# One layer of a hybrid diffusion backbone: w_out with tokens stationary, x2 and its norm token-major

## The chip, the cores and the metric

The kernel runs on one core of a Trainium2 chip. The metric is the device time of one execution in microseconds. It computes in float32; the matrix products use PE's float32r form with each operand split into a high and a low part, so that one product is three matmuls: high by high, high by low, low by high.

## The reference

One layer, run over 128 context tokens and 256 latent tokens (384 together, D = 2048), which share all weights and differ in their modulation vectors. The mixer (attention, Fourier and gating branches, each behind a sigmoid gate) makes `merged`. What the change touches is the rest:

```
x = x + gt1 * rmsnorm(merged @ w_out, g_post_mix)
h = rmsnorm(x, g_pre_mlp) * (1 + sc2) + sh2
ff = square(relu(h @ w1)) @ w2
x = x + gt2 * rmsnorm(ff, g_post_mlp)
```

`sh1, sc1, gt1, sh2, sc2, gt2` come from silu(c) @ w_ada + b_ada: one row for the context, one for the latents.

## The kernel before

The tokens are three tiles of 128. PE gets all its work from one list, `stream`, of weight pieces of 512 KB or 256 KB: SP's queue loads a piece into one of 4 `raw` buffers, ACT makes the high part `whi` (a CAST) and DVE the low part `wlo` (a subtraction), 4 buffers each; `next_half` hands PE one pair of 512 columns and issues the splits for those ahead. "D" pieces go to a function of their own: those of `w_ada` are multiplied on DVE by silu(c) and summed (`ada_dve`), 96 pieces for gt1, sc2 and sh2, spread over the gates and w_out between places `DL` and `DE` of the main list.

There are two block forms. `blockA` holds the weights stationary and moves the 384 tokens (feature-major result, two tiles of 128 features); `blockB` holds a token tile stationary and moves 512 weight columns (token-major result, three token tiles). After each step `slot` issues at most a few waiting small tasks: `late` (evacuations), `urgent` and `side`.

w_out is eight `blockA` (y0 to y7): ACT squares the result, DVE scales it by `a1` = gt1 * g_post_mix (a value per feature, so per partition) into `ya`, and adds the squares. After the last matmul, column sums and the broadcast of 1/rms go through small PE matmuls (`colsum`, `rstd_bc`, tiles r1c, r1d and r). Then each of 16 feature tiles of x2 = x + ya * r1 is made (`x2_a`), split into high and low parts of A2 * x2 (`x2_b`, `x2_c`), and the first three MLP blocks run beside it, k by k. x comes back from DRAM (`spill`), where it was put feature-major early on.

The second norm is not applied to h2: the MLP's first layer multiplies A2 * x2, with the two shift rows `sh2` as two more moving columns (386), and `ff_evac` multiplies by r2 and adds the shift times w1 as the bias of the Relu. For the end of the kernel x2 is transposed back to token-major, one feature tile at a time, as side tasks of the first MLP blocks (`do_x2`, tile px).

The order on each engine is the order in which the code issues instructions; the Tile framework adds the waits.

Of the kernel before, what the change touches and what calls it, by code (L numbers as in the profile page):

```python
# [22 lines left out]
NT = 3  # L23
# [11 lines left out]
def hybrid_layer_kernel(ctx: ExitStack, tc: tile.TileContext, I: dict, O: dict):  # L35
# [132 lines left out]
    a1 = cst.tile([P, 2, 16], F32, name="a1")  # L168
    st = cst.tile([P, 32], F32, name="st")
    ssq3 = cst.tile([P, NT, 4], F32, name="ssq3")  # L170
# [32 lines left out]
    spill = dram.tile([P, 16, TOK], F32, name="spill")  # L203
# [49 lines left out]
    adr = {}  # L253

    def ada_dve(m, j, kk0, on_done, vec):
        def run(raw):
            if (m, j) not in accs:
                if m in (2, 3, 4):
# [48 lines left out]
    def mod_done(m, j):  # L307
# [12 lines left out]
        def fin():  # L320
            dst = modT[:, m, :, s]
            tt(nc.vector, dst.rearrange("p v (h n) -> p v h n", h=2), last.pop("red")[:, 0:256].rearrange("p (n v h r) -> p v h n r", n=2, v=2, h=2)[:, :, :, :, 0],
               bT[:, m, s].rearrange("p (h n) -> p h n", h=2).unsqueeze(1).to_broadcast([P, 2, 2, 2]), ALU.add)
            if m == 2:
                tt(nc.vector, a1[:, :, s], dst, bc2(g_post_mix[:, s]), ALU.mult)
            if m == 4:
                plus1_times(A2, 4, g_pre_mlp, s)

        return lambda: [red, nop, tr, fin]
# [91 lines left out]
    for p in range(8):  # L421
        main += WA(w_out, KT, 256 * p)
    DL, DE = 62, 196
# [3 lines left out]
    for m in (2, 4, 3):  # L427
        for j in range(4):
            dl += ADA(m, j)
    di = 0  # L430
    for i, e in enumerate(main):
# [4 lines left out]
        while di < want:  # L436
            stream.append(dl[di])
            di += 1
# [156 lines left out]
    def mmA(ps, half, k0, src, first, last_, width=TOK, nk=2):  # L595
# [3 lines left out]
        for kk in range(nk):  # L599
            k = k0 + kk  # L600
            xh = src(0, k)[:, 0:width]
            xl = src(1, k)[:, 0:width]
            s0 = first and kk == 0
            s1 = last_ and kk == nk - 1
            for n in range(len(ps)):
                wh = h3[:, kk, n * P:(n + 1) * P]
                wl = l3[:, kk, n * P:(n + 1) * P]
                mm3(ps[n][:, :width], wh, wl, xh, xl, s0, s1)
# [13 lines left out]
    def blockA(name, src, nkt, evac, k_off=0, width=TOK):  # L622
        ps = [acc_tile(f"{name}_{n}") for n in range(2)]
        for k in range(0, nkt, 2):
            h = next_half()
            mmA(ps, h, k_off + k, src, k == 0, k == nkt - 2, width)
# [77 lines left out]
    def spill_x(k):  # L704
        return lambda: nc.scalar.dma_start(out=spill[:, k:k + 2, :], in_=xT[:, k:k + 2, :])

# [7 lines left out]
    n_spill = KT // 2  # L714
    side.extend(spill_x(2 * i) for i in range(n_spill))
# [389 lines left out]
    yx = area.tile([P, 2, 16, TOK], F32, tag="A", name="yx")  # L1105
    ya = yx[:, 0]
    xr = yx[:, 1]
    for k in range(0, KT, 2):
        side.extend([nop] * 5)
        side.append(lambda k=k: nc.sync.dma_start(out=xr[:, k:k + 2, :], in_=spill[:, k:k + 2, :]))  # L1110
    ysum = {}

    def y_sq(p, ps, n):
        def run():
            k = 2 * p + n
            if k == 0:
                ysum["t"] = tp.tile([P, TOK], F32, tag="ta", name="sqa", bufs=1)
                nc.scalar.activation(out=ysum["t"], in_=ps[n][:, :TOK], func=AF.Square)
            else:
                sq = tp.tile([P, TOK], F32, tag="sq", name=f"ysq{k}")  # L1120
                nc.scalar.activation(out=sq, in_=ps[n][:, :TOK], func=AF.Square)
                if k >= KT - 2:
                    ysum["pair"].append(sq)
                else:
                    tt(nc.vector, ysum["t"], ysum["t"], sq, ALU.add)
        return run

    def y_sc(p, ps, n):
        def run():
            k = 2 * p + n  # L1130
            for v, lo, hi in SEG:
                nc.vector.tensor_scalar(out=ya[:, k, lo:hi], in0=ps[n][:, lo:hi], scalar1=a1[:, v, k:k + 1],
                                        scalar2=None, op0=ALU.mult)
        return run

    def y_evac(p):
        return lambda ps: [f(p, ps, n) for f in (y_sq, y_sc) for n in range(2)]

    for p in range(7):
        blockA(f"y{p}", src_m, KT, y_evac(p))  # L1140
    def colsum(pc, sq, first, last_):
        for t in range(NT):
            nc.tensor.matmul(pc[:, t:t + 1], sq[:, t * P:(t + 1) * P], ones[:, 0:1], start=first, stop=last_)
# [12 lines left out]
    ysum["pair"] = []
    for n in range(2):
        for kk in range(2):
            k = KT - 2 + kk
            mm3(ps7[n][:, :TOK], hi[:, kk, n * P:(n + 1) * P], lo[:, kk, n * P:(n + 1) * P], src_m(0, k), src_m(1, k),  # L1160
                False, kk == 1)
        if n:
            tt(nc.vector, ysum["t"], ysum["t"], ysum["pair"][0], ALU.add)
            colsum(pc1[:, 0:NT], ysum["t"], True, True)
            nc.vector.tensor_scalar(out=st[:, 4:7], in0=pc1[:, 0:NT], scalar1=1.0 / D, scalar2=EPS,
                                    op0=ALU.mult, op1=ALU.add)
        y_sq(7, ps7, n)()
    pc2 = mis_tile("r1d")
    colsum(pc2[:, 0:NT], ysum["pair"][1], True, True)
    rsqrt_add(st[:, 0:3], pc2[:, 0:3], st[:, 4:7], 3, D)  # L1170
    for n in range(2):
        y_sc(7, ps7, n)()
    r1 = mis_tile("r1")
    rstd_bc(r1, st[:, 0:3])
    while urgent or side:
        (urgent or side).popleft()()
    assert not delayed and state["done"] >= mlp_start
    h2t = [area.tile([P, 2, 8, 388], F32R, tag="B1", name="h2a"),
           area.tile([P, 2, 4, 388], F32R, tag="B2a", name="h2b"),
           area.tile([P, 2, 4, 388], F32R, tag="B2b", name="h2c")]  # L1180
# [198 lines left out]
```

## Time and profile before

| | |
|---|---|
| median of three runs | 2188.98 us (2188.03 to 2190.05) |
| profiled execution | 2191.05 us, span 2189.3 us |
| PE busy, granted clock | 99%, 0.996 of full |
| DVE, ACT, POOL busy | 63%, 38%, 2% |
| HBM | 178 GB/s over the span |

A matmul's printed duration runs from its start to its result, and the next one starts before that: the pitch is read from one start to the next. The chain of waits goes back from the last instruction and says which engine held the end at each time.

### The profile page before, as it was taken

What the parts mean: (1) busy time and instruction counts of PE and PEld (TensorE: products, weight loads), DVE (VectorE), ACT (ScalarE), POOL (GpSimd) and SP (SyncE); (2) the same over time, 40 slices, a digit from 0 to 9 for tenths busy, and PEclk for the clock granted to TensorE, in tenths of its full rate; (3) what the DMA queues carried; (4) which work ended last, traced back from release to release, by engine and by line L of the source; (5) the groups of instructions that cost most, each with busy time, mean ns of one, the idle gap of its engine ahead of it and who ended that gap; (6) DMA issues with size and microseconds to landing.
All of it is one profiled execution on the core that took longest, in us unless ns stands there. A gap on an engine that the chain in (4) does not pass through costs nothing.

```text
span 2189.3 us, 30886 instructions
## 1 busy us (share of the span) xinstructions
PE 2160.6 (99%) x11647; PEld 1986.8 (91%) x11647; DVE 1374.3 (63%) x2366; ACT 830.5 (38%) x1620; POOL 52.0 (2%) x78
## 2 busy tenths in 40 slices
PE   7999999999999999999999999999999999999998
PEld 3679989999999999999999988999889998899986
DVE  3546765557888878888695666786334444344454
ACT  3333344533333333333355433444333443344341
POOL 0000211000000000000000000000000000000000
PEclk9999999999999999999999999999999999999999
DMA  8897853336667677677634566665444444444352
GB/s 309 283 313 263 249 163 120 106 116 211 205 215 212 206 221 214 207 219 228 189 99 134 156 204 208 202 199 157 135 125 125 126 125 130 131 125 125 126 173 77
DMA packets 285558, 390.47 MB, mean 178 GB/s; under 512 B 16517, under 2 KB 184689, under 8 KB 285025
## 3 DMA queue, kind: packets, MB, share of 16 engines
q1 hardware_dynamic: 275952, 372.82, 54.3%
q0 software_dynamic: 3264, 8.91, 1.5%
q10 hardware_dynamic: 6192, 6.77, 0.9%
q8 instruction: 91, 1.49, 0.3%
q14 instruction: 59, 0.48, 0.1%
HBM read 381.09 MB, written 8.28 MB: 178 GB/s over the span
## 4 chain that ended last, share of the span: by engine, by line
PE 97%; issue 1%; DMA 1%; DVE 1%; ACT 0%; POOL 0%; DVEq 0%; POOLq 0%; ACTq 0%
PE m L592 8%; PE m L593 8%; PE m L591 8%; PE z L614 7%; PE z L616 7%; PE z L615 7%; PE g L591 6%; PE g L593 6%; PE g L592 6%; PE b L591 2%; PE y L591 2%; PE b L593 2%; PE b L592 2%; PE y L592 2%; PE y L593 2%; PE sc L247 2%
## 5 line engine op out<-in xcount | busy, mean ns | idle before, releaser
L64 DVE TENSOR_TENSOR wlo<-raw,whi 128x512 fp32r<-128x512 f32 x908 | 615.9, 690 | 622.9 <-ACT whi L70 619.2
L70 ACT CAST whi<-raw 128x512 fp32r<-128x512 f32 x908 | 559.0, 621 | 996.8 <-PE z L616 282.6
L614 PE MATMUL z<-whi,ff 128*128 128x512 f32 x720 | 280.4, 389 | 0.0
L616 PE MATMUL z<-whi,ff 128*128 128x512 f32 x720 | 280.1, 389 | 0.0
L615 PE MATMUL z<-wlo,ff 128*128 128x512 f32 x720 | 280.1, 389 | 0.0
L591 PE MATMUL g<-hA,whi 128*128 128x384 f32 x768 | 259.0, 337 | 0.0
L593 PE MATMUL g<-hA,wlo 128*128 128x384 f32 x768 | 256.8, 334 | 0.0
L592 PE MATMUL g<-hA,whi 128*128 128x384 f32 x768 | 256.7, 334 | 0.0
L279 DVE SCALAR_TENSOR_TENSOR adr<-raw,silT,adr 128x512 f32<-128x512 f32 x360 | 246.5, 746 | 0.0
L591 PE MATMUL m<-h2a,whi 128*128 128x386 f32 x512 | 175.6, 343 | 2.1 <-ACT h2a L1198 2.1
L592 PE MATMUL m<-h2a,whi 128*128 128x386 f32 x512 | 174.9, 342 | 0.2 <-DVE h2a L1202 0.2
L593 PE MATMUL m<-h2a,wlo 128*128 128x386 f32 x512 | 174.6, 341 | 0.0
L614 PEld LDWEIGHTS z<-whi,ff 128*128 128x128 f32 x720 | 135.1, 188 | 28.7 <-issue 0.8
L616 PEld LDWEIGHTS z<-whi,ff 128*128 128x128 f32 x720 | 135.1, 188 | 28.1
L615 PEld LDWEIGHTS z<-wlo,ff 128*128 128x128 f32 x720 | 135.1, 188 | 27.9
L591 PEld LDWEIGHTS g<-hA,whi 128*128 128x128 f32 x768 | 144.2, 188 | 2.9 <-issue 2.9
L592 PEld LDWEIGHTS g<-hA,whi 128*128 128x128 f32 x768 | 144.2, 188 | 0.0
L593 PEld LDWEIGHTS g<-hA,wlo 128*128 128x128 f32 x768 | 144.2, 188 | 0.0
L591 PEld LDWEIGHTS m<-h2a,whi 128*128 128x128 f32 x512 | 97.7, 191 | 3.3 <-ACT h2a L1198 2.4
L592 PEld LDWEIGHTS m<-h2a,whi 128*128 128x128 f32 x512 | 97.9, 191 | 0.8 <-DVE h2a L1202 0.6
L593 PEld LDWEIGHTS m<-h2a,wlo 128*128 128x128 f32 x512 | 97.5, 190 | 0.0
L592 PE MATMUL m<-h2c,whi 128*128 128x386 f32 x256 | 87.2, 341 | 0.0
(351 smaller groups left out, 3622.1 us busy)
## 6 DMA issues: line engine op xcount, KB each, us to landing
raw<-in_w_mlp_dram SPq DMA_DIRECT2D x244, 512.0 KB, 3.7
raw<-in_w_in_dram SPq DMA_DIRECT2D x156, 512.0 KB, 3.9
raw<-in_w_ada_dram SPq DMA_DIRECT2D x128, 512.0 KB, 4.6
erb<-in_w_ada_dram SPq DMA_DIRECT2D x37, 512.0 KB, 7.1
raw<-in_w_out_dram SPq DMA_DIRECT2D x32, 512.0 KB, 4.4
era<-in_w_ada_dram SPq DMA_DIRECT2D x27, 512.0 KB, 5.2
era<-in_w_in_dram SPq DMA_DIRECT2D x20, 512.0 KB, 5.7
raw<-in_w_br_a_dram SPq DMA_DIRECT2D x16, 512.0 KB, 3.8
```

Source lines behind the costliest of these rows:

```text
L64: eng.tensor_tensor(out=out, in0=a, in1=b, op=op)
L70: nc.scalar.copy(out=hi, in_=full)
L247: nc.tensor.matmul(ps[g:g + 2, :wd], silT[:, :, k], r, start=k < 4, stop=k >= KT - 4)
L279: nc.vector.scalar_tensor_tensor(out=acc[v], in0=r, scalar=vec[:, v, k:k + 1], in1=acc[v], op0=ALU.mult, op1=ALU.add)
L591: nc.tensor.matmul(out, wh, xh, start=start, stop=False)
L592: nc.tensor.matmul(out, wh, xl, start=False, stop=False)
L593: nc.tensor.matmul(out, wl, xh, start=False, stop=stop)
L614: nc.tensor.matmul(ps[t], xh, hi, start=first, stop=False)
L615: nc.tensor.matmul(ps[t], xh, lo, start=False, stop=False)
L616: nc.tensor.matmul(ps[t], xl, hi, start=False, stop=last_)
```

## The change

- **w_out:** three `blockB` of 512 columns (y0 to y2), a block of 256 columns over all tokens (y3), and the last 256 columns (y4) one token tile at a time. Nine tenths of y4's weights are split ahead into a buffer of their own (`y_entry`). ACT sums the squares with its accumulator, DVE multiplies by a1 as a row.
- **a1:** is now needed along the free dimension. After gt1's pieces of a column block are summed, the block is transposed, written to DRAM and read back broadcast over the partitions (`back1`, `back2`, tile a1b). gt1's pieces now come last of the three, and all 96 end eight places earlier (`DE` 188).
- **x:** is loaded token-major from the inputs; the spill is gone.
- **Norms:** x2 is made token-major (`x2_f`), its squares summed, x2 scaled by 1/rms into h2's place (`hn_f`), transposed on PE (`tr_f`) and given scale and shift from per-partition scalars, then split (`ev_f`). x2 is copied by DMA to its own buffer for the end.
- **MLP:** the first layer reads 384 columns; `ff_evac` is a Relu without bias or factor. The first four weight halves are held and used once per token tile with 128 moving columns (`m0`).

The diff, cut to its core:

```diff
-    for p in range(8):
-        main += WA(w_out, KT, 256 * p)
-    DL, DE = 62, 196
+    for n in range(3):
+        main += WB(w_out, 0, KT, 512 * n)
+    main += WA(w_out, KT, 1536)
+    for i in range(3):
+        main.insert(len(main) - 14 + 4 * i, y_entry(4 * i))
+    main.append(("W", w_out, 12, 4, 1792, 256))
+    DL, DE = 62, 188
...
-    for m in (2, 4, 3):
+    for m in (4, 3, 2):
+        if m == 2:
+            dl += [None] * 5
...
+    def y4_fin(t):
+        sq = tp.tile([P, 512], F32, tag="sq", name=f"ysq{t}")
+        nc.scalar.activation(out=sq[:, 0:256], in_=ps4[t], func=AF.Square, accum_out=ssq1[:, t, 4:5])
+        y_sc(ps4[t], t, c4)()
+        rsqrt_add(st[:, t:t + 1], ssq1[:, t, 4:5], st[:, 3 + t:4 + t], 1, D)
+
+    def x2_f(t):
+        for n in range(4):
+            c = slice(512 * n, 512 * (n + 1))
+            nc.vector.scalar_tensor_tensor(out=ya[:, t, c], in0=ya[:, t, c], scalar=st[:, t:t + 1], in1=xr[:, t, c],
+                                           op0=ALU.mult, op1=ALU.add)
+            nc.scalar.activation(out=xr[:, t, c], in_=ya[:, t, c], func=AF.Square, accum_out=ssq2[:, t, n:n + 1])
+
+    def r2_f(t):
+        nc.vector.tensor_reduce(out=st[:, 6 + t:7 + t], in_=ssq2[:, t, :], axis=AX.X, op=ALU.add)
+        rsqrt_mean(st[:, 9 + t:10 + t], st[:, 6 + t:7 + t], 1, D)
+
+    def hn_f(t):
+        for n in range(4):
+            c = slice(512 * n, 512 * (n + 1))
+            nc.scalar.activation(out=xr[:, t, c], in_=ya[:, t, c], func=AF.Copy, scale=st[:, 9 + t:10 + t])
...
+    y4(0, range(KT), True, True)
     flush()
...
+    y4_fin(0)
+    x2_f(0)
+    y4(1, range(KT), True, True)
+    r2_f(0)
+    hn_f(0)
+    y4_fin(1)
+    x2_f(1)
+    k2 = (12, 13, 14, 15) + tuple(range(12))
+    y4(2, k2[:9], True, False)
+    tr_f(0, 0)
+    y4(2, k2[9:], False, True)
...
+    first = [(0, 0), (0, 1), (0, 2), (2, 0)]
+    while len(halves) < len(first):
+        advance()
+    held = [halves.popleft() for _ in first]
+
+    def m0(t):
+        for (k, p), h in zip(first, held):
+            mmA(ps0[p], h, k, src_h2, k == 0 and t == 0, False, slice(t * P, (t + 1) * P))
+
+    ev_f(0, 0)
+    y4_fin(2)
+    x2_f(2)
+    r2_f(1)
+    hn_f(1)
+    m0(0)
+    tr_f(1, 0)
+    ev_f(1, 0)
+    tr_f(0, 1)
+    r2_f(2)
+    hn_f(2)
+    ev_f(0, 1)
+    m0(1)
+    tr_f(2, 0)
+    ev_f(2, 0)
+    tr_f(1, 1)
+    ev_f(1, 1)
+    m0(2)
+    tr_f(2, 1)
+    ev_f(2, 1)
+    for t in range(NT):
+        nc.gpsimd.dma_start(out=x2[:, t, :], in_=ya[:, t, :])
+    fill = deque((t, g) for g in (2, 3) for t in range(NT))
     for k in range(2, KT, 2):
         for p in range(NJ):
+            if (k, p) in first:
+                continue
+            if fill and hn_t:
+                ev_f(*next(iter(hn_t)))
+            mmA(ps0[p], next_half(), k, src_h2, False, k == KT - 2)
+            if fill:
+                tr_f(*fill.popleft())
...
-                blockA(f"m{qd}{p}", src_h2, KT, ff_evac(p), width=386)
+                blockA(f"m{qd}{p}", src_h2, KT, ff_evac(p))
```

How the order moves, first on PE at the hand-over. The order there before (mH and mL are the parts of `merged`, r1c, r1d and r the small matmuls of the norm, h2a the MLP's input):

```order
L593 MATMUL y_1_10049<-mH,wlo_1_10136 128x384
L1143 MATMUL r1c<-ones,sqa 128x1 x3
L1143 MATMUL r1d<-ones,ysq_10207 128x1 x3
L1147 MATMUL r_10219<-ident,st 128x128 x3
L591 MATMUL m_0_10235<-h2a,whi_0_10165 128x386
```

and now, where y4's third token tile ends:

```order
L656 MATMUL y_2_9968<-wyB2b,mH 128x256
L657 MATMUL y_2_9968<-wyB2b,mH 128x256
L658 MATMUL y_2_9968<-wyB2b,mL 128x256
L633 MATMUL m_0_10168<-h2a,whi_0_9956 128x128
L634 MATMUL m_0_10168<-h2a,whi_0_9956 128x128
L635 MATMUL m_0_10168<-h2a,wlo_0_9957 128x128
L633 MATMUL m_1_10169<-h2a,whi_0_9956 128x128
```

The norm's small matmuls are gone from PE, the first four transposes of h stand earlier, 21 matmuls before y4's end, and the first MLP matmuls have 128 columns.

On ACT in the same place, now (ysq and L1199 are the squares of y and x2, L1208 the copies that scale x2, whi the weight splits, h2a the high part of h2):

```order
L1190 ACTIVATE ysq_10029,ssq_95<-y_0_9966 128x256
L1199 ACTIVATE yx,ssq_96<-yx 128x512 x4
L1208 ACTIVATE yx<-yx,st 128x512 x4
L1190 ACTIVATE ysq_10097,ssq_95<-y_1_9967 128x256
L1199 ACTIVATE yx,ssq_96<-yx 128x512 x4
L70 CAST whi_0_10176<-raw_9908 128x512
L70 CAST whi_0_10182<-raw_9954 128x512
L70 CAST h2a<-hf_10186 128x4x128
L1190 ACTIVATE ysq_10193,ssq_95<-y_2_9968 128x256
```

The first high part of h2 stands behind two token tiles of squares, one of copies and two weight splits.

On DVE, the same stretch from the second token tile on (a1b is the a1 row, hf the scaled and shifted h before its split):

```order
L64 TENSOR_TENSOR yx<-y_1_9967,a1b 128x256
L188 SCALAR_TENSOR_TENSOR st<-ssq_95,st 128x1
L1197 SCALAR_TENSOR_TENSOR yx<-yx,st 128x512 x4
L64 TENSOR_TENSOR wlo_0_10177<-raw_9908,whi_0_10176 128x512
L64 TENSOR_TENSOR wlo_0_10183<-raw_9954,whi_0_10182 128x512
L1229 TENSOR_SCALAR hf_10186<-hn_10137,A_92,modT 128x128 x4
L64 TENSOR_TENSOR h2a<-hf_10186,h2a 128x4x128
```

The first h2 group stands behind the second tile's x2 and two low weight parts.

## Rows read from the trace of the kernel before

**Rows 1.** The page, parts 1 and 4: busy time of the engines; the chain of waits.

```profile
PE 2160.6 (99%) x11647; PEld 1986.8 (91%) x11647; DVE 1374.3 (63%) x2366; ACT 830.5 (38%) x1620; POOL 52.0 (2%) x78
...
PE 97%; issue 1%; DMA 1%; DVE 1%; ACT 0%; POOL 0%; DVEq 0%; POOLq 0%; ACTq 0%
```

**Rows 2.** Timeline of PE in w_out (start us, us, engine, line, operation): 25 matmuls.

```profile
1079.75 0.33 PE L591 MATMUL y<-mH,whi 128*128 128x384 f32 x1
...
1083.91 0.33 PE L591 MATMUL y<-mH,whi 128*128 128x384 f32 x1
```

**Rows 3.** The same in the second MLP layer: 28 matmuls.

```profile
2129.67 0.39 PE L615 MATMUL z<-wlo,ff 128*128 128x512 f32 x1
...
2135.79 0.39 PE L615 MATMUL z<-wlo,ff 128*128 128x512 f32 x1
```

**Rows 4.** The same, last quarter of the first MLP layer: its start, its successor.

```profile
1914.13 0.33 PE L591 MATMUL m<-h2a,whi 128*128 128x386 f32 x1
...
2049.86 0.40 PE L614 MATMUL z<-whi,ff 128*128 128x512 f32 x1
```

**Rows 5.** Timeline of the hand-over from w_out to the MLP.

```profile
1095.17 0.34 PE L593 MATMUL y<-mH,wlo 128*128 128x384 f32 x1
...
1098.40 1.65 PE L1147 MATMUL r<-ident,st 128*128 128x128 f32 x6 [1.19 <-POOL st L187]
...
1102.12 0.69 PE L591 MATMUL m<-h2a,whi 128*128 128x386 f32 x1 [2.07 <-ACT h2a L1198]
...
1157.62 0.34 PE L591 MATMUL m<-h2a,whi 128*128 128x386 f32 x1
```

**Rows 6.** Windows: length, busy PE, PEld, DVE, ACT, POOL, granted clock, DMA share, GB/s.

```profile
1098.00:1099.00 1.00, 0.60 (x3) 0.60 (x4) 0.94 (x6) 0.00 (x0) 0.34 (x1) 0.67 0.00 0
...
1107.00:1108.00 1.00, 1.00 (x5) 1.00 (x5) 1.00 (x4) 0.84 (x3) 0.00 (x0) 0.50 0.73 205
...
1109.00:1110.00 1.00, 1.00 (x7) 1.00 (x6) 1.00 (x3) 0.52 (x2) 0.00 (x0) 1.00 0.31 80
```

**Rows 7.** Loads (ns min/median/max), and pieces of the chain with small matmuls (us).

```profile
L288 PEld LDWEIGHTS sum<-adr,ones x96: 106/108/109, 545.9 to 1065.3; 128*32 128x32 f32 x96
...
L591 PEld LDWEIGHTS y<-mH,whi x256: 186/188/189, 958.9 to 1094.7; 128*128 128x128 f32 x128
...
1152.22 0.56 PE r L1143 x6
...
1155.00 0.67 PE r L1147 x6
...
1159.90 0.33 PE px L1245 x3
...
446.03 0.67 PE pg L994 x6
```

**Rows 8.** Timeline of the last norm of the kernel, a chain of the same kind.

```profile
2159.68 0.60 ACT L1260 ACTIVATE zl<-accn 128x512 f32<-128x512 f32 x1 [4.81 <-DVE accn L64]
...
2160.44 0.16 DVE L186 SCALAR_TENSOR_TENSOR st<-ssq,st 128x1 f32<-128x1 f32 x1
...
2160.75 0.57 POOL L187 TENSOR_TENSOR st<-st,mhalf 128x1 f32<-128x1 f32 x1 [654.38 <-DVE st L186]
...
2161.36 2.08 DVE L1330 SCALAR_TENSOR_TENSOR accn<-accn,st,xT 128x512 f32<-128x512 f32 x3 [0.76 <-POOL st L187]
```

**Rows 9.** Groups by line: busy us, mean ns, idle before and its releaser.

```profile
L64 DVE TENSOR_TENSOR wlo<-raw,whi 128x512 fp32r<-128x512 f32 x908 | 615.9, 690 | 622.9 <-ACT whi L70 619.2
...
L1132 DVE TENSOR_SCALAR yx<-y,a 128x128 f32<-128x128 f32 x16 | 5.5, 343 | 0.0
...
L70 ACT CAST whi<-raw 128x512 fp32r<-128x512 f32 x908 | 559.0, 621 | 996.8 <-PE z L616 282.6 <-PE m L592 227.5 <-PE g L592 179.4
```

**Rows 10.** Windows, while the gates run.

```profile
696.00:763.00 67.00, 67.00 (x392) 66.30 (x391) 55.70 (x92) 23.09 (x41) 0.00 (x0) 1.00 0.71 218
```

More of the change, by code (lines that the diff above doesn't have):

```diff
@@ L257, in run @@
             if (m, j) not in accs:
-                if m in (2, 3, 4):
+                if m == 2:
+                    if "t" not in a1bc:
+                        assert not delayed and not urgent
+                        a1bc["t"] = area.tile([P, 2, D], F32, tag="a2", name="a1b")
+                    accs[m, j] = [a1bc["t"][:, v, 512 * j:512 * (j + 1)] for v in range(2)]
+                elif m in (3, 4):
                     if "t" not in adr:
@@ L593, in mm3, with mmA @@
         nc.tensor.matmul(out, wl, xh, start=False, stop=stop)
-    def mmA(ps, half, k0, src, first, last_, width=TOK, nk=2):
+    def mmA(ps, half, k0, src, first, last_, cols=slice(0, TOK), nk=2):
         hi, lo = half
@@ L1103, in hybrid_layer_kernel @@
             blockA(f"b{gi}_{p}", src_o, nk, br_evac(p, gi), k_off=off)
-    yx = area.tile([P, 2, 16, TOK], F32, tag="A", name="yx")
+    yx = area.tile([P, 2, NT, D], F32, tag="A", name="yx")
     ya = yx[:, 0]
     xr = yx[:, 1]
-    for k in range(0, KT, 2):
[L1109 to L1143, printed above, removed]
@@ new lines, in y_sq, with y_sc, run, y_evac @@
+    def y_sq(ps, t, n):
+        return lambda: nc.scalar.activation(out=ps, in_=ps, func=AF.Square, accum_out=ssq1[:, t, n:n + 1])
+    def y_sc(ps, t, c):
+        def run():
+            assert c.start // 512 in a1bc
+            tt(nc.vector, ya[:, t, c], ps, a1bc["t"][:, min(t, 1), c], ALU.mult)
+        return run
+    def y_evac(n, c):
+        w = c.stop - c.start
+        return lambda ps: [f for t in range(NT) for f in (y_sc(ps[t][:, :w], t, c), y_sq(ps[t][:, :w], t, n))]
+    for n in range(3):
+        blockB(f"y{n}", src_m, KT, y_evac(n, slice(512 * n, 512 * (n + 1))))
@@ new lines, in hybrid_layer_kernel @@
+    m0(2)
+    tr_f(2, 1)
+    ev_f(2, 1)
+    for t in range(NT):
+        nc.gpsimd.dma_start(out=x2[:, t, :], in_=ya[:, t, :])
+    fill = deque((t, g) for g in (2, 3) for t in range(NT))
+    for k in range(2, KT, 2):
+        for p in range(NJ):
+            if (k, p) in first:
[5 more added lines that the diff above has]
+                tr_f(*fill.popleft())
+                if not fill:
+                    ev_f(*next(iter(hn_t)))
@@ L1300, in hybrid_layer_kernel @@
     late.popleft()()
-    side.extend(do_x2(k) for k in range(KT))
     for qd in range(4):
```

206 lines of the change are left out of this document (92 added, 114 removed).

## The prediction

> **What bounds the kernel now.** I read the page first. PE is busy 99% of the span and the chain of waits is PE to 97% [rows 1], so only what PE issues, and the places where PE waits, can move the time. Then I read PE's own timeline for the pitch, the step from one matmul's start to the next, because the printed durations overlap. 384 columns: 24 steps in 4.16 us, 0.1733 us each [rows 2]. 512 columns: 27 steps in 6.12 us, 0.2267 us each [rows 3]. The two lie on a line of 0.417 ns a column (2.4 GHz) plus 13.3 ns. 386 columns in the first MLP layer: the 768 matmuls of the last quarter take 135.73 us, 0.1767 us each [rows 4], which is 3.4 ns above 384 columns, not the 0.8 ns of two columns.
>
> Then the one place in the middle where PE waits, the hand-over from w_out to the MLP [rows 5]. The last w_out matmul starts at 1095.17 and its successor would start at 1095.34; the first MLP matmul starts at 1102.12; the first three blocks (288 matmuls, 50.9 us at 0.1767) end where the next block starts, 1157.62. That is 62.3 us for 50.9 us of work, a **loss of 11.4 us**. Part of it is the clock: it falls from full to half (2.4 to 1.2 GHz) at about 1098.7, while PE has only the small r matmuls, and is at full again in 1109, after some six us of MLP matmuls [rows 6].
>
> Last, the two engines that feed PE: DVE is busy 55.70 of 67 us while the gates run, with PE never waiting [rows 10].
>
> **The change part by part.** The sum is against the profiled execution, 2191.05 us with a span of 2189.3; the median of the three runs is 2188.98, 2.07 us lower (0.09%), and I put the same difference on the median. A difference of 0.2%, 4.4 us, is about what a measurement of this kernel can tell from no change.
>
> *w_out.* Removed: 768 matmuls of 384 columns, 133.1 us. Added: 432 of 512 columns, 97.9 us, and 288 of 256 columns. No row shows 256 columns; the line gives 0.120 us, 34.6 us. The upper end is the 384-column row, 0.1733 us, 15 us more. A weight load stands against neither: a 32-column load lasts 108 ns and a 128-column one 188 ns [rows 7], so 128 columns occupy some 107 ns, below 120. I take the line: **-0.6 us**.
>
> *First MLP layer.* 3072 matmuls at 384 instead of 386 columns: 3.4 ns each [rows 2, 4], **-10.2 us**; with the columns alone, 0.8 ns, -2.6 us. I take the first, since the 384-column stage shows the same kind of traffic beside it.
>
> *Transposes.* Gone are 48 transposes of x2 in the MLP (0.33 us for three [rows 7], 5.3 us); new are 48 of h2, at the same 0.111 us. **0.** The column sums and broadcasts of r are inside the 11.4 us.
>
> *a1 as a row.* Four transposes on PE, **+0.5 us**. The round trip through DRAM is issued over 20 us of matmuls before its first reader; DVE gets 12% more modulation work per weight tile in the gates (96 entries over 121 instead of 134 places), some 3.6 us in 67, and had 11 us free [rows 10]. If that cover were gone, late wlo tiles would stop PE. The spill of x through DRAM falls away; six loads of x stand on SP's queue where eight loads of the spill stood, 30 us and more before their first reader. ACT loses Relu pieces and copies in the MLP, off the chain. All 0. The three x2 copies wait on POOL's queue for nothing but x2 itself and have some 45 us until ff is written over their source; if they took longer, ACT's first ff write would hold the weight splits behind it. 0.
>
> *The new hand-over.* I set 0 where the last y3 matmul has been issued and follow the engines' orders. The durations: from a square to the first x2 operation 1.68 us (ACT square, DVE, POOL, DVE), three x2 operations in 2.08 us, 0.67 each [rows 8]; wlo 0.69, CAST 0.62, a 128-column TENSOR_SCALAR from PSUM 0.34 [rows 9]; neighbours on DVE and ACT overlap by some 0.1.
>
> PE has y4 for token tile 0 until 5.8, for tile 1 until 11.5, for tile 2 with four transposes until 17.7. Tile 0: square and norm to 7.5, four x2 operations with their squares to 11.1, norm to 12.1, four copies on ACT to 14.1. ACT runs in order, so tile 1's square starts only there, though y4(1) was ready at 11.5: x2 from 15.8, squares to 19.4. Behind them stand two weight splits (CASTs to 20.4, wlo to 21.3), then the four TENSOR_SCALARs of the first h2 group (22.3) and its CAST (23.0). **PE waits 5.3 us, 17.7 to 23.0.** Then 48 matmuls of 128 columns for tile 0, to 28.9. Tile 1's h2 comes at 31.4, tile 2's at 39.6, by the same chain (transposes, four TENSOR_SCALARs, CAST, wlo): each time PE waits 1.4 us for the high part and 0.6 for the low. The weight splits for the next columns stand behind the last CAST of h2 on ACT: PE waits from 46.0 to 48.4 and 0.5 more. While h2's other half is made, DVE is loaded beyond PE's pace: 1.6 us. Waits in all: 14.6 us.
>
> Matmuls of 128 columns are 144 where 48 of 384 did (8.3 us). No row shows the pitch. Below: the line, 0.067. Nearer: a load with a one-column matmul takes 0.56/6 = 0.093, a load with 128 fp32 columns 0.111 [rows 7]. Above: the whole fp32 matmul of 128 columns, two records, 0.22 [rows 7] (pg). I take 0.111, the row with the same load and the same columns: 16.0 us, 7.7 more. The clock: the wait of 5.3 us is as empty as that of before, so I let the next 5.5 us run at half, where six loads with 128 columns took 1.66 us against 0.67 at full clock [rows 5, 7]: 2.1 us.
>
> The loss is then 14.6 + 7.7 + 2.1 = **24.4 us in place of 11.4**. With 0.067 and no fall of the clock it is 18.6; with every hand-off at its shortest as well, 15.5; with 0.22, 38.
>
> The Trainium skill, page "TensorE: Matmul & The Clock Gate", section "Back-to-back issue gap", gives for streams of loads and matmuls about 81 ns at 128 columns and 131 ns at 512. By it (an estimate from that page) the 144 matmuls take 11.7 us instead of 16.0 and the total would be about 3 us lower. The trace shows 227 ns where the page says 131, so I do not follow it.
>
> **Sum:** -0.6 - 10.2 + 0.5 + (24.4 - 11.4) = +2.7 us: 2193.7 against the profiled 2191.05, and on the median **2191.7 us**, no change that can be told. What the narrower MLP gives back, the hand-over by token tile takes: the first tile's chain hides behind y4(1), but tile 1's does not hide behind anything.
>
> **The rivals.**
> 1. *Slower: 128-column matmuls at 0.22 us.* Place: the 144 matmuls of the first MLP columns. Either they run at the fp32 rate, or the clock stays at half through all three groups, which the waits between them would cause. For: pg's 0.22, the fall at 1098.7 after little PE work [rows 6, 7]. Against: other fp32r matmuls run one column a cycle. Loss 38.4, +16.7: 2205.7 us. It decides from 0.125 us on: there the total leaves the 4.4 us. The Trainium skill, same page, section "HAM oscillation — how this bites in real kernels", has a thin-M kernel whose bursts between waits each start cold; no run here shows repeated falls.
> 2. *The pitch of the MLP stays*, because the 2.6 ns beyond the columns come from ff's traffic, not the width. Gain 2.6 instead of 10.2: +10.3, 2199.3 us. Against: the gates and w_out show 0.1733 beside like traffic.
> 3. *Faster.* 0.067 us a matmul and no fall: loss 18.6, 2185.9; with the shortest hand-offs 15.5, 2182.8 us. For: fp32r at 384 and 512 is on the line. Against: the loads [rows 7].
>
> **How the numbers follow.** Forecast 0.45 (its own range 2187 to 2197, from hand-offs and a pitch of 0.09 to 0.13), rival 1 0.20, rival 2 0.13, rival 3 0.22. Faster by over 0.2%: most of rival 3, 0.19. Within: 0.33 of the forecast and 0.03 of rival 3, 0.36. Slower: 0.12 of the forecast and rivals 1 and 2, 0.45. The range takes in rival 3's end and rival 1: 2183 to 2207.
>
> **What would show it.** On PE's timeline: y0 to y2 at 0.2267, y3 and y4 at 0.120, m at 0.1733 to 0.174 in the last three quarters. After y4's last matmul a PE wait of about 5 us ended by ACT's CAST of h2a, then three groups of 128-column matmuls with waits of 2 us, then 2 to 3 us for whi. From y3's last matmul to the end of the first three MLP blocks 97 us should pass: 17.3 of y4, 5.3 of transposes, 49.9 of MLP matmuls and the loss of 24.4. I am wrong if the 128-column pitch is not near 0.11, if the clock is low for more than some 8 us, if m stays at 0.1767, or if PE waits for wlo in the gates.

## Result and profile after

The changed kernel takes **2224.03 us** (median of 4 runs, 2222.44 to 2226.38), the kernel before 2189.52 (4 runs): 1.0158 times as long, 95% interval 1.014 to 1.0175. The forecast was 2191.7 us, with a range of 2183 to 2207. Since then the kernel before has run in every comparison; its median stayed between 2190.4 and 2191.0 us. The profiled execution of the changed kernel has a span of 2220.7 us against 2189.3, 31.4 us more.

First the page, parts 1, 4 and 5 (busy time of the engines; the chain of waits; one group of matmuls: count, busy time, mean ns, idle time before and its releaser):

```profile
PE 2179.2 (98%) x11669; PEld 1981.5 (89%) x11669; DVE 1332.8 (60%) x2272; ACT 803.5 (36%) x1491; POOL 59.6 (3%) x97
...
PE 92%; DVE 4%; DMA 2%; issue 1%; ACT 1%; POOL 0%; DVEq 0%; POOLq 0%; ACTq 0%
...
L633 PE MATMUL m<-h2a,whi 128*128 128x384 f32 (+1 forms) x544 | 187.5, 345 | 11.6 <-ACT h2a L70 8.5
```

PE still holds 92% of the chain, where it held 97% [rows 1]; DVE and DMA have come in. PE's waits on h2a are 8.5 us. That is far from 31.4, so most of the loss is time in which PE counts as busy. Where it lies comes out of the timelines, stage by stage (from the start of one stage's first matmul to that of the next, in one trace and in the other, us):

| stretch | before | after | difference | predicted |
|---|---|---|---|---|
| start to y0 | 959.1 | 963.6 | +4.5 | 0 |
| y0 to the end of w_out | 136.2 | 139.0 | +2.7 | -0.1 |
| hand-over, from there to the end of the first three MLP blocks | 62.3 | 97.7 | **+35.5** | +17.3 |
| rest of the first MLP quarter | 90.1 | 83.7 | -6.4 | -6.9 |
| from there to the last weight group | 900.1 | 894.7 | -5.3 | -7.8 |
| end | 41.5 | 41.9 | +0.4 | 0 |

The hand-over holds the surprise. The same stretch in windows (us, then for each engine its busy time and count, the granted clock, DMA share, GB/s):

```profile
core 0: us, PE busy (x) PEld busy (x) DVE busy (x) ACT busy (x) POOL busy (x), PEclk, DMA share, GB/s
1098.00:1103.00 5.00, 4.75 (x42) 4.55 (x40) 2.04 (x5) 3.04 (x9) 0.54 (x1) 1.00 0.00 0
1103.00:1108.00 5.00, 0.00 (x0) 0.00 (x0) 3.70 (x8) 2.97 (x8) 0.00 (x0) 0.86 0.11 28
1108.00:1113.00 5.00, 3.99 (x18) 3.81 (x18) 3.66 (x8) 2.73 (x8) 0.54 (x1) 0.50 0.22 77
1113.00:1118.00 5.00, 5.00 (x25) 5.00 (x25) 0.44 (x3) 3.54 (x8) 0.54 (x1) 0.50 0.00 0
...
1138.00:1143.00 5.00, 5.00 (x25) 5.00 (x25) 1.40 (x4) 0.62 (x1) 0.00 (x0) 0.50 0.00 0
1143.00:1148.00 5.00, 5.00 (x25) 5.00 (x25) 0.00 (x0) 0.00 (x0) 0.00 (x0) 0.50 0.00 0
1148.00:1153.00 5.00, 2.37 (x9) 1.67 (x8) 3.63 (x8) 2.18 (x4) 0.00 (x0) 0.50 0.00 0
1153.00:1158.00 5.00, 5.00 (x30) 4.94 (x29) 1.92 (x6) 0.97 (x2) 0.00 (x0) 0.86 0.48 157
```

The clock falls to half (1.2 GHz) while PE waits in 1103 to 1108, as it did before [rows 6]. It then stays at 0.50 for some 48 us, also in 1113 to 1118 and 1138 to 1148, where PE is busy all the time. It rises only in 1153 to 1158, behind the first matmuls of 384 columns. PE's own timeline (start us, us, engine, line, operation, count, idle time before):

```profile
1084.08 0.28 PE L658 MATMUL y<-whi,mL 128*128 128x256 f32 x1
1084.20 0.28 PE L656 MATMUL y<-whi,mH 128*128 128x256 f32 x1
...
1108.76 0.48 PE L633 MATMUL m<-h2a,whi 128*128 128x128 f32 x1 [6.01 <-ACT h2a L70]
1109.48 0.47 PE L634 MATMUL m<-h2a,whi 128*128 128x128 f32 x1 [0.25 <-DVE h2a L64]
...
1110.19 0.41 PE L634 MATMUL m<-h2a,whi 128*128 128x128 f32 x1
1110.40 0.41 PE L635 MATMUL m<-h2a,wlo 128*128 128x128 f32 x1
...
1151.28 0.69 PE L633 MATMUL m<-h2a,whi 128*128 128x384 f32 x1 [2.63 <-ACT whi L70]
```

The 256-column step is the 0.120 us that the line gave. The wait ahead of the first MLP matmul is 6.0 us (5.3 predicted), those ahead of the other groups 1.25 (1.4 predicted), the one for whi 2.63 (2.4 predicted). The 128-column step is 0.213 us where 0.111 was taken; each group of 48 lasts 10.8 us.

### The profile page after: what moved, and what is told of

Its sections match the earlier page's. It is cut to its first block, busy times and chain, and to the rows that moved or that the text cites. A ratio compares the mean times of both kernels' runs of the same rounds, so it can differ in the third digit from the quotient of the medians.

```text
span 2220.7 us, 30737 instructions
## 1 busy us (share of the span) xinstructions
PE 2179.2 (98%) x11669; PEld 1981.5 (89%) x11669; DVE 1332.8 (60%) x2272; ACT 803.5 (36%) x1491; POOL 59.6 (3%) x97
## 4 chain that ended last, share of the span: by engine, by line
PE 92%; DVE 4%; DMA 2%; issue 1%; ACT 1%; POOL 0%; DVEq 0%; POOLq 0%; ACTq 0%
PE m L634 8%; PE m L635 8%; PE m L633 8%; PE z L656 7%; PE z L657 7%; PE z L658 7%; PE g L633 6%; PE g L635 6%; PE g L634 6%; PE b L633 2%; PE b L634 2%; PE b L635 2%; PE sc L248 2%; PE y L657 2%; PE y L656 2%; PE y L658 2%
## 5 line engine op out<-in xcount | busy, mean ns | idle before, releaser
L633 PE MATMUL m<-h2a,whi 128*128 128x384 f32 (+1 forms) x544 | 187.5, 345 | 11.6 <-ACT h2a L70 8.5
L634 PE MATMUL m<-h2a,whi 128*128 128x384 f32 (+1 forms) x544 | 186.5, 343 | 0.8 <-DVE h2a L64 0.8
L635 PE MATMUL m<-h2a,wlo 128*128 128x384 f32 (+1 forms) x544 | 186.7, 343 | 0.4 <-DVE wlo L64 0.4
L286 DVE SCALAR_TENSOR_TENSOR adr<-raw,silT,adr 128x512 f32<-128x512 f32 x240 | 164.2, 744 | 0.0
L656 PEld LDWEIGHTS z<-whi,ff 128*128 128x128 f32 x720 | 135.2, 188 | 28.7 <-issue 0.8
L658 PEld LDWEIGHTS z<-whi,ff 128*128 128x128 f32 x720 | 135.2, 188 | 28.1
L657 PEld LDWEIGHTS z<-wlo,ff 128*128 128x128 f32 x720 | 135.2, 188 | 27.8
L633 PEld LDWEIGHTS m<-h2a,whi 128*128 128x128 f32 x544 | 109.5, 201 | 14.2 <-ACT h2a L70 9.5
L634 PEld LDWEIGHTS m<-h2a,whi 128*128 128x128 f32 x544 | 109.4, 201 | 1.4 <-DVE h2a L64 1.3
L635 PEld LDWEIGHTS m<-h2a,wlo 128*128 128x128 f32 x544 | 109.5, 201 | 1.3 <-DVE wlo L64 1.3
L633 PE MATMUL m<-h2b,whi 128*128 128x384 f32 x256 | 86.6, 338 | 0.4 <-ACT whi L70 0.4
```

The costliest lines, as they stand in the source:

```text
L286: nc.vector.scalar_tensor_tensor(out=acc[v], in0=r, scalar=vec[:, v, k:k + 1], in1=acc[v], op0=ALU.mult, op1=ALU.add)
L633: nc.tensor.matmul(out, wh, xh, start=start, stop=False)
L634: nc.tensor.matmul(out, wh, xl, start=False, stop=False)
L635: nc.tensor.matmul(out, wl, xh, start=False, stop=stop)
L656: nc.tensor.matmul(ps[t], xh, hi, start=first, stop=False)
L657: nc.tensor.matmul(ps[t], xh, lo, start=False, stop=False)
```

## The experiments

Three theories of the 0.213 us went into the first runs: **A**, this stream of 128-column matmuls does not bring the clock back once it is at half; **B**, such a matmul costs 0.213 us at any clock; **C**, the waits between the groups keep the clock low. All runs are of the changed kernel with the edit named, where nothing else is said.

### Width alone: e1_wide and e2_nogap

Both move the first MLP group behind the third token tile's h2; one issues it at 384 columns, the other as three times 128 without a wait between.

```diff
-    m0(0)
...
-    m0(1)
...
-    m0(2)
+    m0()
```

This is e1_wide, where `m0` runs `mmA` over all 384 columns; in e2_nogap the last line is `m0(t)` for the three tiles in turn.

> The changed kernel with the first MLP group done once, 48 matmuls of 384 columns after all three token tiles have their first h2 group, in place of three times 48 of 128 columns. PE then waits longer (estimate from the changed kernel's orders and durations: from 1102.6 to about 1125 us), but no narrow matmul is left. Theory A (a stream of 128-column matmuls does not bring the granted clock back from half): the clock returns to 1.00 within some 6 us of the first 384-column matmul, as in the kernel before, the group takes about 11 us and ends near 1136, 11 us ahead of the changed kernel: about 2213 us. Theory B (128 columns cost 0.213 us at any clock): the same, since none is left. Theory C (the waits between the groups keep the clock low, the width does not matter): the same too; the pair with the next run tells A and B from C. If none of them holds and only the chain of waits counts, the longer wait makes it slower: about 2236 us.

> The same as the run before it, but the group is done as three times 48 matmuls of 128 columns, one behind the other without a wait between them; the only difference to that run is the width. Theory A: the clock stays at 0.50 through all 144 matmuls, 0.213 us each, 30.7 us; the group ends near 1156 us in the trace, 8 us behind the changed kernel: about 2232 us. Theory C (waits between the groups kept it low): the clock returns to 1.00 after some 6 us and the rest runs at about 0.107 us each: about 19 us, end near 1144: about 2220 us. Theory B: 0.213 us each with the granted clock back at 1.00, 2232 us.

Measured: e1_wide 2211.71 us (2211.45 to 2213.1), e2_nogap 2228.66 (four runs: 2229.39, 2228.66, 2228.67 and 2217.81). Windows of e1_wide; its first 384-column matmul starts at 1125.8:

```profile
1123.00:1128.00 5.00, 2.16 (x6) 1.76 (x7) 3.93 (x10) 0.93 (x3) 0.00 (x0) 0.50 1.01 413
1128.00:1133.00 5.00, 5.00 (x20) 5.00 (x19) 0.69 (x1) 0.40 (x1) 0.00 (x0) 0.62 0.17 70
1133.00:1138.00 5.00, 4.79 (x30) 4.51 (x28) 0.17 (x1) 0.00 (x0) 0.00 (x0) 1.00 0.00 0
```

and of e2_nogap; its 128-column matmuls run from 1123.1 to 1153.9 without a gap:

```profile
1123.00:1128.00 5.00, 5.00 (x26) 5.00 (x25) 3.50 (x9) 1.40 (x3) 0.00 (x0) 0.50 1.00 401
1133.00:1138.00 5.00, 5.00 (x25) 5.00 (x25) 0.00 (x0) 0.00 (x0) 0.00 (x0) 0.50 0.02 3
1148.00:1153.00 5.00, 5.00 (x25) 5.00 (x25) 0.00 (x0) 0.00 (x0) 0.00 (x0) 0.50 0.00 0
1158.00:1163.00 5.00, 5.00 (x20) 4.60 (x20) 1.85 (x5) 0.56 (x2) 0.00 (x0) 0.57 0.48 157
```

The two edits differ in the width alone (the wide group waits for all three token tiles and so starts 2.7 us later). With 384 columns the clock is back within some 6 us, with 128 it stays at 0.50 for 30.8 us of unbroken work. C falls: there are no waits in that stretch. e1_wide is 12 us faster than the changed kernel although PE waits longer in it. The execution of e2_nogap at 2217.81 has a mean granted clock of 0.991 against 0.986 to 0.987 in the other three, so the clock seems to have come back early in that one; there is no trace of it. In three of four executions the narrow stream left the clock at half.

The Trainium skill, page "TensorE: Matmul & The Clock Gate", Part 1 on the clock gate, says that the warm-up is a stretch of time and not a number of matmuls, and gives an example with 128 columns. By it the clock would have come back in e2_nogap's 30.8 us as it did in e1_wide. The trace does not agree, and decides.

### The same width at full clock: e3_steady

```diff
+    N3 = tuple(slice(t * P, (t + 1) * P) for t in range(NT))
+    N2 = (slice(0, 256), slice(256, 384))
+    PARTS = {(1, 2): N3, (1, 3): N3, (1, 4): N3, (2, 2): N2, (2, 3): N2, (2, 4): N2}
...
-            mmA(ps, h, k_off + k, src, k == 0, k == nkt - 2)
+            for i, c in enumerate(parts):
+                mmA(ps, h, k_off + k, src, k == 0 and i == 0, k == nkt - 2 and i == len(parts) - 1, c)
```

> The changed kernel with three blocks of the second MLP quarter as three times 128 columns (864 matmuls in place of 288) and three blocks of the third quarter as 256 and 128 columns (576 in place of 288), in the middle of full-clock streams with no wait around them. Pitch of 128 columns at full clock 0.107 us (half of the 0.213 us seen at half clock, as weight loads bound it) if A or C holds and the clock stays: the three blocks take 92 us in place of 50, the other three 65 in place of 50, about 2281 us in all. If the narrow stream by itself lets the clock fall (a strong form of A), the first three run at 0.213 us with granted clock 0.50, 184 us: about 2373 us. Theory B (0.213 us at granted clock 1.00): about 2373 us too, told apart by the clock.

Measured: 2283.42 us (one run). The stretch of 128 columns in the timeline, its first and last rows, and in windows:

```profile
1448.48 0.22 PE L633 MATMUL m<-h2a,whi 128*128 128x128 f32 x1
1448.54 0.28 PE L634 MATMUL m<-h2a,whi 128*128 128x128 f32 x1
1448.65 0.27 PE L635 MATMUL m<-h2a,wlo 128*128 128x128 f32 x1
...
1545.62 0.39 PE L633 MATMUL m<-h2a,whi 128*128 128x384 f32 x1
```

```profile
1460.00:1480.00 20.00, 20.00 (x181) 20.00 (x181) 7.91 (x14) 3.10 (x5) 0.00 (x0) 1.00 0.41 124
1500.00:1520.00 20.00, 20.00 (x182) 20.00 (x181) 6.11 (x9) 3.87 (x7) 0.00 (x0) 1.00 0.35 105
```

864 matmuls take 97.1 us, **0.112 us each at granted clock 1.00**; the eight small matmuls of another sum stand among them, without a wait. B falls, and so does the strong form of A: started at full clock, this unbroken narrow stream kept it. The 0.111 us taken in the prediction from a load of 128 columns was the right price at full clock. The 576 matmuls of 256 and 128 columns in the third quarter ran at 1.00 too, 66.1 us.

### Keeping PE at work: e4_warm

```diff
+    def warm(n):
+        pw = mis_tile(f"warm{n}")
+        for i in range(n):
+            nc.tensor.matmul(pw, held[0][0][:, 0:P], held[0][0], start=i == 0, stop=i == n - 1)
...
+    warm(24)
     m0(0)
...
+    warm(9)
     m0(1)
...
+    warm(9)
     m0(2)
```

> The changed kernel with matmuls of 512 columns on resident weights, their sums unused, put on PE ahead of the three groups of 128 columns: 24 ahead of the first and 9 ahead of each other, so that PE works through its waits. Nothing else is changed. Theory A: the clock is kept up (1.00), the 144 matmuls run at about 0.107 us (15.4 us in place of 30.7), the chain of tile 2 then sets the last group (start near 1125, end near 1130 us in place of 1147.6), and the first 384-column matmuls behind it run at full clock: about 2205 us. Theory B: 0.213 us each with clock 1.00, no gain: 2224 to 2227 us. Theory W (the chain of waits alone makes the loss, whatever the clock): 2220 to 2227 us.

Measured: 2210.84 us median (2209.34, 2209.45, 2212.22, 2221.39), 13 us less than the changed kernel. Windows:

```profile
1103.00:1108.00 5.00, 5.00 (x27) 4.21 (x26) 3.70 (x8) 3.75 (x10) 0.00 (x0) 1.00 0.00 0
1118.00:1123.00 5.00, 5.00 (x36) 4.59 (x37) 2.19 (x7) 3.37 (x6) 2.15 (x4) 1.00 0.39 144
1128.00:1133.00 5.00, 5.00 (x39) 4.68 (x38) 2.66 (x6) 0.66 (x2) 0.00 (x0) 1.00 0.17 72
1138.00:1143.00 5.00, 4.81 (x19) 4.32 (x20) 2.39 (x5) 1.18 (x3) 0.00 (x0) 0.66 0.42 128
```

With useless work in the waits the clock stays at 1.00 and the groups take 5.3 to 6.2 us instead of 10.8, as theory A expected. The clock falls once more at the wait for whi, in 1138 to 1143. The 2205 us expected were too low: waits of 0.6, 0.4, 1.0, 1.0 and 2.6 us and that fall stayed. (The execution at 2221.39 has a mean clock of 0.991 against 0.995 to 0.997, so there it seems to have been lost after all; there is no trace of it.)

### The two smaller losses: e6_early

```diff
-    DL, DE = 62, 188
+    DL, DE = 62, 196
...
+    side.extend([nop] * 8)
     side.extend([load_cache(ckn, "cache_k"), load_cache(cv, "cache_v")])
```

> The changed kernel with the two edits of the earlier stages undone: eight empty places in the side queue where the spill's eight stores stood, and the modulation spread over 134 places (end 196) instead of 126 (end 188). The changed kernel's first y matmul starts 4.5 us late, and PE waits for raw weights at 1022 us with the clock down to 0.69 behind it, some 4 us. If the side queue's shift and the denser modulation are the cause: y0 starts near 960 and the wait at 1022 is gone or smaller, 2216 to 2220 us. If the loss lies in the width of y or in the a1 row's round trip, which both stay: no change, 2222 to 2226 us. The trace tells the two edits apart: the empty places act between 187 and 467 us, the spread behind it.

Measured: 2223.56 us, no change. The two edits work against each other in the trace. With the eight empty places the last branch blocks of the first gate group start at 465.75 instead of 468.06. The wider spread brings waits for wlo of 3.1 us in the gates (0.8 in the changed kernel) and of 3.0 us in w_out (1.7), and y0 starts at 962.76, 0.8 us earlier. (e8_full, below, has the empty places without the wider spread, and waits 0.8 us in the gates as the changed kernel does: the 3.1 us belong to the spread.) The changed kernel's own wait in w_out, and the steps of 0.43 us at half clock behind it:

```profile
1022.82 0.50 PE L656 MATMUL y<-whi,mH 128*128 128x512 f32 x1 [0.52 <-ACT whi L70]
1024.47 0.62 PE L657 MATMUL y<-wlo,mH 128*128 128x512 f32 x1 [1.15 <-DVE wlo L64]
1024.89 0.63 PE L658 MATMUL y<-whi,mL 128*128 128x512 f32 x1
```

### The first MLP layer alone: e5_before384, e10_stride, e12_pitch400

These are edits of the kernel before. e5_before384 and e10_stride leave the shift term out of the computation, so they show a time and are no replacement.

```diff
-            mmA(ps0[p], next_half(), k, src_h2, k == 0, k == KT - 2, 386)
+            mmA(ps0[p], next_half(), k, src_h2, k == 0, k == KT - 2)
...
-                blockA(f"m{qd}{p}", src_h2, KT, ff_evac(p), width=386)
+                blockA(f"m{qd}{p}", src_h2, KT, ff_evac(p))
```

e10_stride adds rows of `TOK` (384) in place of 388 columns for h2, without the writes of the shift's columns; e12_pitch400 has the 386 columns of before and only `[P, 2, 8, 400]` for h2a.

> The kernel before, with the two columns of the shift left out of the first MLP layer (384 columns instead of 386, and the shift term replaced by columns of the product, so that part of the computation is left out); nothing else is changed, and the reads of the other 384 columns are not moved. This is the term 'first MLP layer' alone. As predicted (3.4 ns for each of 3072 matmuls): 10.2 us faster, 2179 to 2180 us. By the changed kernel's last quarters (133.94 us for 768 matmuls against 135.73, 2.3 ns each): 7.2 us faster, 2182 to 2183 us. By the two columns alone: 2.6 us faster, 2187 us.

> The kernel before with 384 columns in the first MLP layer as in e5_before384 (the shift term left out of the computation), and h2 stored at 384 columns a row instead of 388, without the shift's columns. e5_before384 gained 1.0 us a quarter (1.35 ns a matmul), the changed kernel 1.8 us a quarter (2.3 ns). If the row pitch of h2 makes the rest: 133.9 us in the last quarter, about 2183 us. If the rest comes from the work beside it (evacuations, bias, transposes of x2): 134.7 us and 2186 to 2187 us as in e5_before384.

> The kernel before with the rows of the first half of h2 (h2a) 400 columns apart instead of 388, that is 1600 bytes instead of 1552; 386 columns are read as before, and the result is the same. In e10_stride, 384 in place of 388 took the step of the matmuls on h2a from 175.2 to 173.4 ns at equal width, and left those on h2b and h2c nearly as they were. If it is the row's place (1536 bytes is a multiple of 64, 1552 is not, 1600 is): the steps on h2a go from 176.9 to about 175.2 ns, those on h2b and h2c stay at 175.8 and 177.2, 1536 matmuls, 2.7 us: about 2187.7 us. If it is something else about 384: 176.9 ns and 2190.4 us.

Measured: 2186.61, 2183.80 and 2188.32 us, against 2190.4 to 2191.0; ratios 0.998 (0.997 to 0.999), 0.9968 (0.9957 to 0.9979), 0.999 (0.9981 to 0.9999). The mean step from the start of one matmul to the next start in the last two quarters, in ns:

| | h2a (k 0 to 7) | h2b | h2c |
|---|---|---|---|
| before: 386 columns, rows of 388 | 176.9 | 175.9 | 177.2 |
| e5: 384, rows of 388 | 175.1 | 175.3 | 176.0 |
| e10: 384, rows of 384 | 173.5 | 176.0 | 174.7 |
| changed kernel | 173.5 | 176.0 | 174.7 |
| e12: 386, h2a in rows of 400 | 175.9 | 175.7 | 177.2 |

e10 and the changed kernel agree in every column. The last quarter of e10, its first matmul and its successor, is 133.94 us as in the changed kernel (135.73 before [rows 4], 134.70 in e5):

```profile
1907.92 0.33 PE L591 MATMUL m<-h2a,whi 128*128 128x384 f32 x1
...
2041.86 0.39 PE L614 MATMUL z<-whi,ff 128*128 128x512 f32 x1
```

e5's 4.4 us lie between the two columns' 2.6 and the 7.2 that the changed kernel shows. The rest of what the changed kernel gains comes from where the rows lie, as e10 and e12 show: in rows of 400, h2a loses 1.0 ns a step (1.7 expected) with the width unchanged. On 1536 matmuls that is 1.5 us; the medians of e12_pitch400 and the kernel before are 2.1 us apart, just clear of no difference.

### Taking the waits out: e7_order, e9_orderwarm, e8_full, e11_best

e7_order issues the same hand-over work in another order. Its core (`x2_p`, `sx_p`, `hn_p`, `ts_p`, `hi_p`, `lo_p` are single pieces of `x2_f`, `hn_f` and `ev_f`):

```diff
+    y4(1, (12, 13, 14, 15), True, False)
+    y4(2, (12, 13, 14, 15), True, False)
+    while len(halves) < 4:
+        advance()
+    hn_p(0, 0)
+    y4(1, range(12), False, True)
+    tr_f(0, 0)
+    y4(2, range(12), False, True)
     y4_fin(1)
...
+    m0(0, 0, 1, 2)
     tr_f(1, 0)
+    m0(0, 3)
...
+    m0(2, 0)
     tr_f(1, 1)
+    advance()
```

e9_orderwarm adds `warm(5)` ahead of the second and third group, and moves two sets of transposes one block later. e8_full adds the eight empty places, `y_entry` at `len(main) - 10 + 4 * i`, and the rest of h2 in every second block. e11_best puts `hn_p(0, 2)` ahead.

> The changed kernel with the same work in the hand-over, in another order: the first h copy of a tile alone (not all four) ahead of the next tile's square, the last k tiles of y4 for tiles 1 and 2 ahead so that the weight splits come early, the next weight splits ahead of the last h2 parts, transposes put between the blocks of 128 columns. No width is changed: three groups of 128 columns. By the engines' orders and the durations of the trace PE waits 0 to 1 us before each group instead of 6.0, 1.25 and 1.25. Theory A (a clock that never falls stays up under 128 columns, 0.107 to 0.11 us each): granted clock 1.00 through the hand-over, the groups end near 1121 us instead of 1147.6, the wait of 2.6 us for the next weights and the half-clock block behind it go too: about 2193 us (2190 to 2198). If the clock falls all the same, the 144 matmuls run at 0.213 us: 2205 to 2212 us. If the waits were put down wrongly and the chain is longer than its rows: 2210 to 2224 us.

> The reordered hand-over of the run before (e7_order) with 5 matmuls of 512 columns on resident weights, sums unused, ahead of the second and of the third group of 128 columns, to fill the waits of 0.2, 0.8 and 0.4 us there, after which the granted clock fell from 1.00 to 0.50 in that run and stayed there for the 84 matmuls that followed; two transposes stand one block later to free a PSUM buffer for them. Theory A (small gaps inside a stream of narrow matmuls let the clock fall, and the narrow stream then cannot raise it): clock 1.00 through all three groups, 96 matmuls at 0.11 in place of 0.215 us (10 us), the transposes and the first 384-column block at full clock (2.6 us): about 2193 us. If narrow matmuls with transposes between them lose the clock by themselves, whatever the gaps: 2206 to 2208 us.

> e9_orderwarm plus three edits elsewhere: the eight empty places in the side queue (attention stage, 2 to 4 us by the trace of e6_early), the three resident w_out weight tiles split five entries later in the weight stream (away from the modulation, the wait at 1022 us, about 3 us), and the rest of h2 made in every second block instead of every block, with the weight split ahead of h2's own low part on DVE (the waits of 0.2 to 0.5 us in the blocks behind the hand-over, about 3 us). By the sum about 2185 us (2181 to 2191), a version that could beat both kernels; if the clock falls in it, some 10 us more. Each edit is read from its own stretch of the trace.

> e8_full with one h copy put ahead on ScalarE (the copy that the first transposes behind the narrow groups read; in e8_full PE waits 2.3 us for it at 1121 us, since it stands behind two casts). Nothing else is changed. If that wait goes: 2.3 us less than e8_full, 2187.5 to 2188 us, against 2190.4 for the kernel before: within 0.2% of it or just faster. If the cast of the last h2 part then ends later and PE waits for that: no change, 2190 us.

Measured: e7_order 2206.26 us (2201.49 to 2207.73), e9_orderwarm 2199.35 (2196.09 to 2200.81), e8_full 2190.03 (11 runs), **e11_best 2187.32** (11 runs, 2185.58 to 2189.22; 0.9987 of the kernel before, interval 0.9978 to 0.9996). e7_order in windows, and the rows of PE's timeline where its clock falls:

```profile
1103.00:1108.00 5.00, 5.00 (x48) 5.00 (x46) 4.29 (x11) 3.15 (x11) 1.24 (x2) 1.00 0.02 3
1108.00:1113.00 5.00, 3.58 (x28) 3.16 (x27) 3.73 (x8) 3.29 (x8) 0.31 (x1) 0.91 0.00 0
1113.00:1118.00 5.00, 5.00 (x25) 5.00 (x25) 0.53 (x3) 3.28 (x6) 2.15 (x4) 0.50 0.40 147
```

```profile
1110.79 0.27 PE L635 MATMUL m<-h2a,wlo 128*128 128x128 f32 x1
1111.88 0.33 PE L633 MATMUL m<-h2a,whi 128*128 128x128 f32 x1 [0.82 <-ACT h2a L1265]
1112.61 0.47 PE L634 MATMUL m<-h2a,whi 128*128 128x128 f32 x1 [0.39 <-DVE h2a L64]
...
1113.09 0.41 PE L633 MATMUL m<-h2a,whi 128*128 128x128 f32 x1
```

The wait of 6 us is gone and the first group runs at full clock. Then the clock falls at 1112.1 (0.91 over the window from 1108), right behind a gap of 0.82 us in front of the second group and ahead of the next one, of 0.39; before these PE had waited only once in the hand-over, for 0.20 us. It stays at 0.50 to the end of the stream, 1136, and comes back behind the first 384 columns. In e9_orderwarm ten 512-column matmuls stand in front of the second and third group, and the gaps left are of 0.2 to 0.3 us:

```profile
1113.00:1118.00 5.00, 5.00 (x45) 4.92 (x45) 1.68 (x6) 2.90 (x7) 2.16 (x4) 1.00 0.58 210
1118.00:1123.00 5.00, 4.70 (x40) 4.36 (x38) 2.06 (x5) 0.88 (x2) 0.00 (x0) 1.00 0.99 410
```

The clock stays at 1.00 through the groups (all four executions of e9_orderwarm have a mean clock of 0.998 or 0.999, those of e7_order 0.992 to 0.994), and the stretch from the start of the last w_out matmul to the end of the first three blocks goes from 80.4 to 72.8 us (97.9 in the changed kernel, 62.5 before). In e11_best it is 67.8 us, at full clock throughout:

```profile
1100.00:1105.00 5.00, 4.54 (x34) 4.01 (x34) 3.38 (x7) 3.37 (x10) 0.00 (x0) 1.00 0.00 0
1110.00:1115.00 5.00, 4.72 (x40) 4.37 (x38) 2.06 (x5) 0.88 (x2) 0.00 (x0) 1.00 0.99 413
```

The wait at 1022 us is gone too (no wait of PE in w_out; y0 to the last w_out matmul 135.2 us, 138.9 in the changed kernel). The hand-over is still 5.4 us longer than before; the shorter MLP pays for it. e8_full came out 5 us above the sum expected, e9_orderwarm 6. Both kept a wait of 2.3 us for a copy on ACT, right behind the groups (in e9 the clock fell there once more, 0.66 in 1130 to 1135), which neither sum had; e11_best takes it away and gains 2.7 us (2.3 expected). The rest of the excess stays open.

## Why the prediction was wrong

The step that failed is **the clock in "the new hand-over"**: "I let the next 5.5 us run at half" (2.1 us). The duration of that fall was taken from the kernel before, where 386-column matmuls ended it after six us [rows 6]. Here the matmuls behind the wait had 128 columns, and the half clock lasted until matmuls of 384 columns came, 42 us after the first of the narrow ones. The three groups took 32.4 us where 16.0 of matmuls and 1.8 of waits for low parts (three of 0.6) had been put: +14.6. The 20 transposes between the groups, also at half, took some 2 us more than at full clock, and the first 384-column block 3.7 us instead of 2.1: together some 18 us where 2.1 had been allowed. That is rival 1 in its second form ("the clock stays at half through all three groups"). But the reason given there, the waits between the groups, is not borne out: in e2_nogap there are none, and the clock stays at half. That the price, a loss of 38.4 us, comes near the 42.5 measured (1085.28 to 1200.33 is 115.05, less 17.3, 5.3 and 49.9) is in part luck: it was worked out from 0.22 us, the fp32 rate of pg, and 0.213 us at half clock happens to lie beside it. The rival was given 0.20, and it was argued against only in its first form, the fp32 rate; nothing was said against the second.

Point by point:

- **w_out** at 0.2267 and 0.120 us: right. But PE waited 1.7 us there for weight splits, and the clock fell to half behind it, which I had at 0: +2.7 us instead of -0.1. With the resident tiles split later the waits are gone (e8_full, e11_best), and the wider spread of e6_early does not take them away. What the loads of x add was not taken apart.
- **Start to y0**, not in the sum at all: +4.5. Some 2.3 of it is the side queue: the spill's eight stores had held eight places ahead of the attention's tasks, which now come earlier (e6_early puts the places back). The rest lies in the gates, where wlo is late for 0.8 us, a sign that the prediction named, and one of three sums that stood in w_out has moved in.
- **First MLP layer**: -7.2 us (2.33 ns for each of 3072) instead of -10.2. The 0.1733 us of [rows 2] is a short undisturbed stretch, the 0.1767 of [rows 4] a mean over a quarter; the changed kernel's mean is 0.1744 (133.94 us for 768). Of the 1.1 ns of gain that was not there, 0.4 come from the short stretch: 240 matmuls of 384 columns in w_out before (976.69 to 1018.22) have a mean of 0.1737. The other 0.7 are h2's own steps, 173.5, 176.0 and 174.7 ns in the table above. Rival 2 was right that the whole 3.4 ns would not come, though not by its reason, ff's traffic: e10_stride keeps that traffic and has the changed kernel's steps.
- **The waits** were right within a microsecond: 6.0, 1.25 and 2.6 us for 5.3, 1.4 and 2.4.
- **128 columns**: 0.111 was right at full clock (0.112 in e3_steady) and wrong where it stood.
- **Small slips.** The clock before fell at 1098.3, not 1098.7: 0.67 over [rows 6]'s window from 1098 means half clock for its last 0.66 us. 5.5 us at half by the row named (1.66 us for 0.67) lose 3.3 us, not 2.1. Rival 3's 18.6 does not follow from the terms shown (24.4 less 2.1 less 6.3 for the shorter step is 16.0); longer waits may make the difference, but the text does not work them out.
- The upper end, 2207, was rival 1 alone. The 7 us ahead of the hand-over and the 3 us of the MLP came on top, and no case held them.

## What to carry to other kernels

Behind a wait, price the matmuls that follow at half clock until a run shows what brings the clock back, and not only the wait itself. Here 384 columns brought it back and 128 mostly did not, so wide matmuls belong behind the wait and narrow ones where nothing has let the clock fall. If narrow matmuls must follow a wait, a handful of wide ones in the wait, their sums unused, can pay for themselves (13 us for 42 of them in e4_warm, 7 us for 10 in e9_orderwarm, where two sets of transposes moved as well). Compare pitches only over stretches of the same kind, a mean with a mean.

## What the runs showed of the hardware

- The granted clock of a narrow stream depended on where it began: 144 matmuls of 128 columns, unbroken for 30.8 us, ran at 0.50 when they began at half (the traced execution of e2_nogap), and 864 of them, unbroken for 97.1 us, at 1.00 when they began at full (e3_steady). In e7_order it fell from full right behind a gap of 0.8 us in such a stream; with wide matmuls in place of the gap it stayed (e9_orderwarm). What makes it fall or rise is not settled by these runs: one execution in four of e2_nogap and of e4_warm seems to have gone the other way, and the wait of 2.3 us right behind the groups let the clock fall in the trace of e9_orderwarm and not in that of e8_full (1.00 from 1100 to 1160 us).
- Where the rows of the moving operand lie counts: at 384 columns a step on h2a takes 175.1 ns with rows of 1552 bytes (e5) and 173.5 with rows of 1536 (e10); at 386 columns 176.9 with 1552 (before) and 175.9 with 1600 (e12). h2b did not follow (175.3 with 1552, 176.0 with 1536), so the row pitch is not the whole of it; what else sets it was not tried.
